# Row sums at the end of a summed-area diagonal kernel: folds on TensorE, weight matmuls on top of an early scan, and fewer load pieces

## The chip, the cores and the metric

One Trainium2 chip; the program runs on one of its cores. The metric is device microseconds of one execution. The timed executions of one kernel agree within about 0.5%; a profiled execution also gives a *span*, the part that the profile covers, about 1.7 to 2 us shorter than the timed value. In the profile PE is TensorE, PEld its weight loads, DVE VectorE, ACT ScalarE, POOL GpSimd and SP SyncE. HBM is the chip's main memory; SBUF and PSUM are memories on the core, and the matmuls of this kernel write to PSUM. Every run told here is of the undisturbed (fast) state.

## The reference

```python
def setup_inputs():
    B, H, W = 4, 4224, 4224
    return {"x": np.random.randn(B, H, W).astype(np.float32)}

def reference(x):
    ps = np.cumsum(np.cumsum(x, axis=1), axis=2)
    diag = np.diagonal(ps, axis1=1, axis2=2)
    return np.cumsum(diag, axis=1).astype(np.float32)
```

The output is tiny (4 x 4224 numbers), but its last value sums over a whole image, so all 285 MB of x must be read once.

## The kernel before

Each of the four images is loaded in strips of 384 rows (3 rows on each of 128 partitions), cast to bf16 by the load. The increment of the diagonal of the summed-area table at index i is a column sum above the diagonal plus a row sum left of it. Column sums come from TensorE (a selector matmul into `d`). Row sums are shared by ScalarE (a copy with an accumulator) and VectorE (a reduce), and are added to `d` through an identity matmul. Two scans of `d` along its 384 columns, a carry between the groups, and y is stored.

The last image is special, because what follows the last load cannot be hidden. Its strips g = 8 and g = 9 arrive in pieces, and the last 384 rows are treated apart: their block near the diagonal is loaded at the very start (`head_a`, `head_b`), the rest (`strip`, 256 rows; `tail`, 128 rows) comes last. Only after the 256 rows' sums are in `d_last` can the two scans over the last 384 rows run.

```python
    DUMP = 2176
    CUTS = {NG - 3: (2176,), NG - 2: (2176, 768)}   # pieces of strips g = 8 and g = 9
# ... cut: constants, scans, between, the loop over the strips
        for q in range(F):
            matmul(d[:ng, q : GW : F], rows[:, :ng, q], ident)
        c12 = smalls.tile([NG, 2, GW], FP32, name="c12")
        scans(d[:ng, :], ng, GW, 0.0, 0.0, c12)
# ... cut: carry matmuls, and lcarry, the carry into the last 384 rows
        cuts = [(1920, T0), (640, 1920), (0, 640)]
        for c0, c1 in cuts:
            nc.gpsimd.dma_start(out=strip[:, :2, c0:c1], in_=src[:, :, c0:c1])
# ... cut: tail pieces
        between(b, ng, c12, carry_ps)                # y of the first ten groups, on VectorE
        lsa = last.tile([P, 3, 2], FP32, name="lsa")
        for i, (c0, c1) in enumerate(cuts):
            act_sum(lsa[:, i, 0:1], strip[:, 0, c0:c1])
            nc.vector.reduce_sum(
                out=lsa[:, i, 1:2], in_=strip[:, 1, c0:c1], axis=AX.X
            )
            for q in range(2):
                matmul(d_last[:, q : 2 * P : 2], lsa[:, i, q : q + 1], ident)

        lc = last.tile([1, 2, GW], FP32, name="lc")
        scans(d_last, 1, GW, lcarry[:, 0:1], lcarry[:, 1:2], lc)
# ... cut: store of 256 values, sums of the tail's pieces into tsum
        nc.vector.reduce_sum(out=ttot, in_=tsum, axis=AX.X)
        matmul(fin, ttot, wtri, start=True)          # the last 128 rows enter by weights
        nc.vector.tensor_add(out=yl, in0=fin, in1=lc[:, 1, 2 * P : GW])
        nc.sync.dma_start(out=out[b, TB:N].unsqueeze(0), in_=yl)
```

Of the kernel before, what the change touches and what calls it, by code (L numbers as in the profile page):

```python
# [17 lines left out]
def kernel(  # L18
# [36 lines left out]

    TB = N - P
    T0 = N - GW
    HB = 2 * P
    head_a = last.tile([P, 2, GW], FP32, name="head_a")
    nc.sync.dma_start(  # L60
        out=head_a, in_=x[LB, T0:TB, T0:N].rearrange("(p f) w -> p f w", f=2)
    )
    head_b = last.tile([P, HB], FP32, name="head_b")
    nc.sync.dma_start(out=head_b, in_=x[LB, TB:N, N - HB : N])

    def load_group(b, g, cuts=()):

        t = strips.tile([P, F, N], BF16, name="strip")
        r0 = g * GW
        src = x[b, r0 : r0 + GW, :].rearrange("(p f) w -> p f w", f=F)  # L70
        hi = N
        for lo in (*cuts, 0):
            if cuts:
                nc.gpsimd.dma_start(out=t[:, :, lo:hi], in_=src[:, :, lo:hi])  # L74
            else:
                nc.gpsimd.dma_start(out=t, in_=src)  # L76
            hi = lo
        return t
# [12 lines left out]
    def upper_masks(f, w):  # L91
# [63 lines left out]
    wtri_i = consts.tile([P, P], I32, name="wtri_i")  # L155
    nc.gpsimd.iota(wtri_i, pattern=[[1, P]], base=1, channel_multiplier=-1)
    wtri = consts.tile([P, P], FP32, name="wtri")
    nc.gpsimd.tensor_copy(out=wtri, in_=wtri_i)
    nc.gpsimd.affine_select(
        out=wtri,  # L160
        in_=wtri,
        compare_op=ALU.is_ge,
        fill=0.0,
        base=0,
        pattern=[[1, P]],
        channel_multiplier=-1,
    )
# [10 lines left out]
    CUTS = {NG - 3: (2176,), NG - 2: (2176, 768)}  # L178
# [12 lines left out]

    hs = last.tile([P, 3], FP32, name="hs")
    hu = last.tile([P, 3], FP32, name="hu")
    hrow = last.tile([P, 3], FP32, name="hrow")
    hmu_a = last.tile([P, 2, GW], BF16, name="hmu_a")
    hmu_b = last.tile([P, P], BF16, name="hmu_b")
    nc.vector.reduce_sum(out=hs[:, 0:2], in_=head_a, axis=AX.X)
    nc.vector.reduce_sum(out=hs[:, 2:3], in_=head_b, axis=AX.X)  # L198
    for k, o, i, m in (
        (0, hmu_a[:, 0, :], head_a[:, 0, :], um2[0]),  # L200
        (1, hmu_a[:, 1, :], head_a[:, 1, :], um2[1]),
        (2, hmu_b, head_b[:, HB - P : HB], um1),
    ):
        nc.vector.scalar_tensor_tensor(
            out=o,
            in0=i,
            scalar=1.0,
            in1=m,
            op0=ALU.mult,
            op1=ALU.mult,  # L210
            accum_out=hu[:, k : k + 1],
        )
    nc.vector.tensor_sub(out=hrow, in0=hs, in1=hu)
# [19 lines left out]
    def between(b, ng, c12, carry_ps):  # L233
        carry = smalls.tile([NG, 2], FP32, name="carry")
        nc.vector.tensor_copy(out=carry[:ng, :], in_=carry_ps[:ng, :])
        y = smalls.tile([NG, GW], FP32, name="y")
        nc.vector.tensor_scalar(
            out=y[:ng, :],
            in0=step[:ng, :],
            scalar1=carry[:ng, 0:1],  # L240
            scalar2=carry[:ng, 1:2],
            op0=ALU.mult,
            op1=ALU.add,
        )
        nc.vector.tensor_add(out=y[:ng, :], in0=y[:ng, :], in1=c12[:ng, 1, :])  # L245
        nc.sync.dma_start(
            out=out[b, : ng * GW].rearrange("(g i) -> g i", i=GW), in_=y[:ng, :]
        )

    for b in range(B):  # L250
# [23 lines left out]
        if not whole:  # L274
            for q in range(2):
                columns(NG - 1, 0, GW, hmu_a[:, q, :])
            columns(NG - 1, GW - P, GW, hmu_b)
            for q in range(2):
                matmul(d_last[:, q : 2 * P : 2], hrow[:, q : q + 1], ident)
# [6 lines left out]
        def sum_pieces(g, parts):  # L286
            nc.vector.reduce_sum(out=rs[:, g, :], in_=parts, axis=AX.X)
            nc.vector.tensor_sub(out=rows[:, g], in0=rs[:, g], in1=ru[:, g])

        for g in range(ng):  # L290
            lo, hi = g * GW, (g + 1) * GW
            cuts = () if whole else CUTS.get(g, ())
            strip = prefetched.pop((b, g), None)
            if strip is None:
                strip = load_group(b, g, cuts)
            if cuts:
                n_parts = 2 * len(cuts) + 2
                parts = last.tile([P, F, n_parts], FP32, name=f"parts{g}")
                c0 = cuts[0]
                ws = c0 + (lo - c0) * 5 // 8 // 32 * 32  # L300
                sa_at = lambda q: parts[:, q, 0:1]
                rs_at = parts[:, :, 1]
            else:
                c0, ws = 0, scalar_cols(g)
                sa_at = lambda q: sa[:, g, q : q + 1]
                rs_at = rs[:, g, :]
            for j in range(g + 1, NG):
                for q in range(F):
                    columns(j, 0, GW, strip[:, q, j * GW : (j + 1) * GW])
            for q in range(F):  # L310
                mu = mup.tile([P, GW], BF16, name="mu")
                nc.vector.scalar_tensor_tensor(  # L312
                    out=mu,
                    in0=strip[:, q, lo:hi],
                    scalar=1.0,
                    in1=um3[q],
                    op0=ALU.mult,
                    op1=ALU.mult,
                    accum_out=ru[:, g, q : q + 1],
                )  # L320
                columns(g, 0, GW, mu)
                if ws > c0:
                    act_sum(sa_at(q), strip[:, q, c0:ws])
            nc.vector.reduce_sum(out=rs_at, in_=strip[:, :, ws:hi], axis=AX.X)  # L324
            if not cuts:
                continue
            k = 2
            for p0, p1 in zip((*cuts[1:], 0), cuts):
                ws = p0 + (p1 - p0) // 2
                for q in range(F):  # L330
                    act_sum(parts[:, q, k : k + 1], strip[:, q, p0:ws])
                nc.vector.reduce_sum(  # L332
                    out=parts[:, :, k + 1], in_=strip[:, :, ws:p1], axis=AX.X
                )
                k += 2
            if g == ng - 2:
                sum_up(0, g)
            sum_pieces(g, parts)

        if whole:  # L340
            sum_up(0, ng)
        for q in range(F):
            matmul(d[:ng, q : GW : F], rows[:, :ng, q], ident)

# [3 lines left out]
        carry_ps = psum_s.tile([NG, 2], FP32, name="carry_ps")  # L348
        matmul(carry_ps[:ng, :], earlier[:ng, :ng], c12[:ng, :, GW - 1], start=True)
        matmul(carry_ps[:ng, 1:2], apart[:ng, :ng], c12[:ng, 0, GW - 1 : GW])  # L350
        if whole:
            between(b, ng, c12, carry_ps)
# [3 lines left out]
        lcarry_ps = psum_s.tile([1, 2], FP32, name="lcarry_ps")  # L356
# [4 lines left out]

        src = x[b, T0:TB, :].rearrange("(p f) w -> p f w", f=2)
        strip = strips.tile([P, F, N], BF16, name="strip")
        cuts = [(1920, T0), (640, 1920), (0, 640)]
        for c0, c1 in cuts:
            nc.gpsimd.dma_start(out=strip[:, :2, c0:c1], in_=src[:, :, c0:c1])  # L366
        tail = strips.tile([P, F, N], BF16, name="strip")
        tcuts = [(2432, N - HB), (1024, 2432), (384, 1024), (0, 384)]
        for c0, c1 in tcuts:
            nc.gpsimd.dma_start(out=tail[:, 0, c0:c1], in_=x[b, TB:N, c0:c1])  # L370

        between(b, ng, c12, carry_ps)

        lsa = last.tile([P, 3, 2], FP32, name="lsa")
        for i, (c0, c1) in enumerate(cuts):
            act_sum(lsa[:, i, 0:1], strip[:, 0, c0:c1])
            nc.vector.reduce_sum(  # L377
                out=lsa[:, i, 1:2], in_=strip[:, 1, c0:c1], axis=AX.X
            )
            for q in range(2):  # L380
                matmul(d_last[:, q : 2 * P : 2], lsa[:, i, q : q + 1], ident)

        lc = last.tile([1, 2, GW], FP32, name="lc")
        scans(d_last, 1, GW, lcarry[:, 0:1], lcarry[:, 1:2], lc)
        nc.sync.dma_start(out=out[b, T0:TB].unsqueeze(0), in_=lc[:, 1, : 2 * P])

        tsum = last.tile([P, 7], FP32, name="tsum")
        nc.vector.tensor_copy(out=tsum[:, 6:7], in_=hrow[:, 2:3])
        fold = psum_s.tile([P, 2 * P], FP32, name="fold")  # L390
        for c0 in range(tcuts[0][0], tcuts[0][1], 2 * P):
            matmul(
                fold,
                ident_h,
                tail[:, 0, c0 : c0 + 2 * P],
                start=c0 == tcuts[0][0],
            )
        nc.vector.reduce_sum(out=tsum[:, 0:1], in_=fold, axis=AX.X)
        k = 1
        for (c0, c1), ws in zip(tcuts[1:], (640, 256, 0)):  # L400
            if ws:
                act_sum(tsum[:, k : k + 1], tail[:, 0, c0 : c0 + ws])
                k += 1
            nc.vector.reduce_sum(  # L404
                out=tsum[:, k : k + 1], in_=tail[:, 0, c0 + ws : c1], axis=AX.X
            )
# [38 lines left out]
```

## Time and profile before

| | before |
|---|---|
| time, median of 3 | 672.1 us (671.86 to 672.22; a fourth run, made later, took 674.20) |
| span of the profiled execution | 670.5 us |
| read from HBM | 285.47 MB, 426 GB/s over the span |
| one strip lands every | 14.95 us, 434 GB/s |
| loads end | 664.25 us (the windows' last quarter with traffic) |
| VectorE / TensorE / ScalarE busy | 39% / 34% / 23% |

The page's line of the HBM traffic (bytes and mean rate):

```profile
HBM read 285.47 MB, written 0.07 MB: 426 GB/s over the span
```

The load stream bounds the kernel for the first 650 us. What a change to the compute can win lies after the last strip. This is the timeline there (start us, duration us, engine, source line, operation, output<-inputs, count, and in brackets the idle time before it and what ended it). L377 are the row sums of the 256 rows, L216 and L224 the two scans over the last 384 rows, L404 the sums of the last 128 rows, L409 their total:

```profile
652.75 1.45 PE L173 MATMUL d<-ident,rows 128*10 128x128 f32 x6 [8.19 <-DVE rows L288]
...
657.90 4.25 DVE L377 TENSOR_REDUCE lsa<-strip 128x1 f32<-128x1920 bf16 x3
...
662.96 1.00 DVE L216 TENSOR_TENSOR_SCAN lc<-ones_row,lcarry,d_last 1x384 f32<-1x384 f32 x1 [0.80 <-PE d_last L173]
...
664.00 1.00 DVE L224 TENSOR_TENSOR_SCAN lc<-ones_row,lcarry,lc 1x384 f32<-1x384 f32 x1
...
665.31 1.85 DVE L404 TENSOR_REDUCE tsum<-strip 128x1 f32<-128x768 bf16 x3
667.26 0.16 DVE L409 TENSOR_REDUCE ttot<-tsum 128x1 f32<-128x7 f32 x1
...
667.57 0.59 PE L173 MATMUL fin<-wtri,ttot 128*1 128x128 f32 x2 [3.38 <-DVE ttot L409]
668.19 0.28 DVE L413 TENSOR_TENSOR yl<-fin,lc 1x128 f32<-1x128 f32 x1 [0.77 <-PE fin L173]
```

VectorE works in one chain from 657.9 to 667.4. Its one wait is the 0.80 us before the first scan, in which TensorE adds VectorE's own last row sums to `d_last`. From the total (667.26) to the end of the span pass 3.2 us.

The windows of the same stretch (start:end, length, busy us and instructions of each engine, granted TensorE clock as a share of full speed, DMA share, GB/s):

```profile
core 0: us, PE busy (x) PEld busy (x) DVE busy (x) ACT busy (x) POOL busy (x), PEclk, DMA share, GB/s
...
658.50:661.90 3.40, 1.43 (x7) 0.58 (x8) 3.40 (x3) 1.76 (x4) 0.00 (x0) 0.50 1.09 208
661.90:665.30 3.40, 2.29 (x11) 1.03 (x9) 2.56 (x5) 1.34 (x4) 0.00 (x0) 0.70 0.34 56
665.30:668.70 3.40, 0.59 (x2) 0.11 (x2) 2.30 (x6) 0.00 (x0) 0.00 (x0) 0.80 0.00 0
```

The clock is at half in the first of these windows, released in the course of the second and back at half near the end of the third.

### The profile page before, as it was taken

The page shows a single profiled execution, that of the slowest core. Times are in us where ns is not written, and L with a number is a line of the kernel's source. Part 1 is how long each engine was busy: PE and PEld are TensorE (multiplying, and loading weights), DVE is VectorE, ACT ScalarE, POOL GpSimd, SP SyncE. Part 2 cuts the span into 40 slices and gives each one's busy share as a digit, 9 for nine tenths or more (in the row PEclk, how much of TensorE's full clock was granted, in tenths as well). Part 3 has the DMA queues.
Part 4 walks back from the last instruction along what each step waited for, and adds up shares of the span by engine and source line. Part 5 has one row for each costly group of instructions (what it writes and reads, how often), then busy time and mean ns, then how long its engine had stood idle before and what let it go on. Part 6 is the DMA issues. An engine that isn't in the chain of part 4 may idle for free.

```text
span 670.5 us, 2653 instructions
## 1 busy us (share of the span) xinstructions
PE 226.3 (34%) x860; PEld 96.0 (14%) x860; DVE 261.3 (39%) x374; ACT 155.7 (23%) x263; POOL 35.4 (5%) x73
## 2 busy tenths in 40 slices
PE   0444443211145543221125543222214533332313
PEld 0211211000022211100012221110002211111101
DVE  2223334344613333334472222333456222233767
ACT  0001222233301112223330111222342011122553
POOL 5000000000000000000000000000000010000100
PEclk9977766555577766566557766766655776766656
DMA  9999999999999999999999999999999999999996
GB/s 199 220 218 217 218 218 218 216 218 218 215 218 218 218 217 216 215 216 216 215 216 217 216 218 218 216 216 218 217 216 219 216 218 217 218 216 206 215 212 114
DMA packets 9814, 143.22 MB, mean 214 GB/s; under 512 B 925, under 2 KB 2250, under 8 KB 4554
## 3 DMA queue, kind: packets, MB, share of 16 engines
q0 software_dynamic: 9296, 142.48, 99.6%
q1 hardware_dynamic: 506, 0.59, 0.3%
q8 instruction: 6, 0.10, 0.1%
q14 instruction: 6, 0.05, 0.0%
HBM read 285.47 MB, written 0.07 MB: 426 GB/s over the span
## 4 chain that ended last, share of the span: by engine, by line
another core or an unknown queue 67%; ACT 22%; DMA 7%; DVE 2%; issue 1%; PE 1%; POOL 0%; ACTq 0%; DVEq 0%; POOLq 0%
ACT dump L183 22%; DMA strip<-in_x_dram 7%; DVE lsa L377 1%; DVE tsum L404 0%; PE d L173 0%; PE d_last L173 0%; POOL strip L76 0%; DVE lc L216 0%; DVE lc L224 0%; DVE c L224 0%; DVE c L216 0%; ACTq L183 0%; PE fin L173 0%; DVE y L245 0%
## 5 line engine op out<-in xcount | busy, mean ns | idle before, releaser
L173 PE MATMUL d<-strip,sel 128*11 128x384 bf16 x630 | 174.7, 457 | 346.0 <-DMA strip<-in_x_dram 346.0
L183 ACT ACTIVATE dump<-strip 128x640 bf16<-128x640 bf16 (+14 forms) x131 | 142.3, 1086 | 508.1 <-DMA strip<-in_x_dram 505.3
L312 DVE SCALAR_TENSOR_TENSOR mu<-strip,um 128x384 bf16<-128x384 bf16 x129 | 65.2, 555 | 374.1 <-DMA strip<-in_x_dram 374.1
L173 PEld LDWEIGHTS <-sel 128*11 128x11 bf16 (+1 forms) x792 | 90.2, 114 | 519.1 <-issue 497.1
L324 DVE TENSOR_REDUCE rs<-strip 128x3 f32<-128x1152 bf16 (+10 forms) x41 | 158.2, 3858 | 0.0
L173 PE MATMUL d<-mu,sel 128*11 128x384 bf16 x129 | 38.1, 404 | 40.6 <-DVE mu L312 40.6
L76 POOL DMA_DIRECT2D strip<-in_x_dram x41 | 22.0, 539 | 509.8 <-PE d L173 240.8
L183 ACT ACTIVATION_READ_ACCUMULATOR dump<-strip 128x1 f32 x131 | 24.4, 186 | 0.0
L173 PE MATMUL d<-ident,rows 128*11 128x128 f32 (+1 forms) x24 | 5.8, 414 | 28.1 <-DVE rows L284 19.9
L173 PE MATMUL d_last<-strip,sel 128*1 128x384 bf16 x30 | 9.0, 425 | 12.1 <-DMA strip<-in_x_dram 12.1
L312 DVE DVE_READ_ACCUMULATOR mu<-strip,um 128x1 f32 x129 | 10.6, 82 | 0.0
L332 DVE TENSOR_REDUCE parts<-strip 128x3 f32<-128x3264 bf16 (+2 forms) x3 | 7.3, 2421 | 5.0 <-DMA strip<-in_x_dram 5.0
L173 PEld LDWEIGHTS d<-ident,rows 128*11 128x11 f32 (+1 forms) x24 | 2.7, 127 | 32.6 <-DVE rows L284 15.0
L216 DVE TENSOR_TENSOR_SCAN c<-ones_row,d 11x384 f32<-11x384 f32 (+1 forms) x4 | 3.8, 942 | 6.3 <-PE d L173 6.3
L74 POOL DMA_DIRECT2D strip<-in_x_dram x5 | 3.8, 762 | 34.5 <-PE d L173 27.3
L198 DVE TENSOR_REDUCE hs<-head_b 128x1 f32<-128x256 f32 x1 | 0.4, 419 | 13.0 <-DMA head_b<-in_x_dram 13.0
L324 DVE TENSOR_REDUCE parts<-strip 128x3 f32<-128x2208 bf16 (+1 forms) x2 | 5.3, 2650 | 0.0
L366 POOL DMA_DIRECT2D strip<-in_x_dram x3 | 2.1, 713 | 42.7 <-DMA strip<-in_x_dram 42.7
L377 DVE TENSOR_REDUCE lsa<-strip 128x1 f32<-128x1920 bf16 (+2 forms) x3 | 4.3, 1465 | 0.0
L173 PE MATMUL d_last<-ident,lsa 128*1 128x128 f32 x12 | 3.0, 406 | 3.3 <-DVE lsa L377 3.0
L224 DVE TENSOR_TENSOR_SCAN c<-ones_row,c 11x384 f32<-11x384 f32 (+1 forms) x4 | 3.8, 946 | 0.1
L173 PE MATMUL carry_ps<-c,earlier 11*11 11x2 f32 (+1 forms) x8 | 0.7, 159 | 8.4 <-DVE c L224 8.4
(62 smaller groups left out, 35.8 us busy)
## 6 DMA issues: line engine op xcount, KB each, us to landing
strip<-in_x_dram POOLq DMA_DIRECT2D x41, 3168.0 KB, 82.7
strip<-in_x_dram POOLq DMA_DIRECT2D x2, 1536.0 KB, 76.0
strip<-in_x_dram POOLq DMA_DIRECT2D x1, 1632.0 KB, 83.2
strip<-in_x_dram POOLq DMA_DIRECT2D x1, 1056.0 KB, 80.1
strip<-in_x_dram POOLq DMA_DIRECT2D x1, 960.0 KB, 64.3
strip<-in_x_dram POOLq DMA_DIRECT2D x1, 640.0 KB, 52.7
strip<-in_x_dram POOLq DMA_DIRECT2D x1, 576.0 KB, 74.9
head_a<-in_x_dram SPq DMA_DIRECT2D x1, 384.0 KB, 3.7
```

The costliest lines, as they stand in the source:

```text
L74: nc.gpsimd.dma_start(out=t[:, :, lo:hi], in_=src[:, :, lo:hi])
L76: nc.gpsimd.dma_start(out=t, in_=src)
L173: nc.tensor.matmul(o, lhsT=lhsT, rhs=rhs, start=start, stop=False, skip_group_check=True)
L183: nc.scalar.activation(out=dump[:, :w], in_=src, func=ACT.Copy, accum_out=acc)
L198: nc.vector.reduce_sum(out=hs[:, 2:3], in_=head_b, axis=AX.X)
L216: nc.vector.tensor_tensor_scan(out=c12[:rows, 0, :width], data0=ones_row[:rows, :width], data1=d, initial=init1, op0=ALU.mult, op1=ALU.add,)
L224: nc.vector.tensor_tensor_scan(out=c12[:rows, 1, :width], data0=ones_row[:rows, :width], data1=c12[:rows, 0, :width], initial=init2, op0=A ...
L312: nc.vector.scalar_tensor_tensor(out=mu, in0=strip[:, q, lo:hi], scalar=1.0, in1=um3[q], op0=ALU.mult, op1=ALU.mult, accum_out=ru[:, g, q ...
L324: nc.vector.reduce_sum(out=rs_at, in_=strip[:, :, ws:hi], axis=AX.X)
L332: nc.vector.reduce_sum(out=parts[:, :, k + 1], in_=strip[:, :, ws:p1], axis=AX.X)
L366: nc.gpsimd.dma_start(out=strip[:, :2, c0:c1], in_=src[:, :, c0:c1])
L377: nc.vector.reduce_sum(out=lsa[:, i, 1:2], in_=strip[:, 1, c0:c1], axis=AX.X)
```

## The change

The intent: get the last rows' scans off the end. They now run early, on what is known without the late row sums; those enter afterwards through matmuls with fixed weights (`w2`, `w1`), because the double cumulative sum is linear and a row sum at row r adds (i + 1 - r) times itself to index i. The row sums themselves are shared by three engines: TensorE folds wide blocks into 160 or 256 columns by identity matmuls, ScalarE and VectorE take the rest. Strips g = 8 and g = 9 arrive whole, the end in 5 pieces instead of 7; the 256 rows' near-diagonal block (`diag_a`) comes in after strip g = 0 of the last image; y of the first ten groups moves to GpSimd.

The core of the diff, cut (the load helper, the constants and the bookkeeping are left out):

```diff
     DUMP = 2176
-    CUTS = {NG - 3: (2176,), NG - 2: (2176, 768)}
# ... cut
+            if not whole and g == ng - 1:
+
+                wp, ws = 1280, 1280 + 1536
+                fold9 = psum_s.tile([P, F, 160], FP32, name="fold")
+                fold_in(fold9, strip, 0, wp, 160)
# ... cut: diag_a and its sums at g == 0 and g == 1
+            fold_a = psum_s.tile([P, 2, 256], FP32, name="fold_a")
+            A_SHARES = [(768, 1152), (768, 640)]
+            (c0, c1), (wp, wa) = acuts[0], A_SHARES[0]
+            fold_in(fold_a, strip[:, :2], c0, c0 + wp, 256)
# ... cut: ScalarE's and VectorE's shares of the first piece
-        between(b, ng, c12, carry_ps)
-
-        lsa = last.tile([P, 3, 2], FP32, name="lsa")
-        for i, (c0, c1) in enumerate(cuts):
-            act_sum(lsa[:, i, 0:1], strip[:, 0, c0:c1])
-            nc.vector.reduce_sum(
-                out=lsa[:, i, 1:2], in_=strip[:, 1, c0:c1], axis=AX.X
-            )
-            for q in range(2):
-                matmul(d_last[:, q : 2 * P : 2], lsa[:, i, q : q + 1], ident)
-
+        between(b, ng, c12, carry_ps, nc.gpsimd)
         lc = last.tile([1, 2, GW], FP32, name="lc")
         scans(d_last, 1, GW, lcarry[:, 0:1], lcarry[:, 1:2], lc)
# ... cut: second piece of the 256 rows
+        nc.vector.reduce_sum(out=asum[:, :, 5], in_=fold_a, axis=AX.X)
+        arows = last.tile([P, 2], FP32, name="arows")
+        nc.vector.reduce_sum(out=arows, in_=asum, axis=AX.X)
# ... cut
+        for q in range(2):
+            ar = arows[:, q : q + 1]
+            matmul(fin_b, ar, w2[q][:, 2 * P : GW], start=q == 0)
+            matmul(fin_a, ar, w2[q][:, 0 : 2 * P], start=q == 0)
# ... cut: sums of the tail into tsum
         nc.vector.reduce_sum(out=ttot, in_=tsum, axis=AX.X)
-        matmul(fin, ttot, wtri, start=True)
-        yl = last.tile([1, P], FP32, name="yl")
-        nc.vector.tensor_add(out=yl, in0=fin, in1=lc[:, 1, 2 * P : GW])
-        nc.sync.dma_start(out=out[b, TB:N].unsqueeze(0), in_=yl)
+        matmul(fin_b, ttot, w1)
+        yl = last.tile([1, GW], FP32, name="yl")
+        for fin, c0, c1 in ((fin_a, 0, 2 * P), (fin_b, 2 * P, GW)):
+            nc.vector.tensor_add(out=yl[:, c0:c1], in0=fin, in1=lc[:, 1, c0:c1])
+            nc.sync.dma_start(
+                out=out[b, T0 + c0 : T0 + c1].unsqueeze(0), in_=yl[:, c0:c1]
+            )
```

## The prediction

> **What bounds it now.** The load stream. The page's HBM line: 285.47 MB read, 426 GB/s over the span. The timeline shows one full strip (384 rows, 6.49 MB of fp32) landing every 14.95 us (590.1, 605.04, 620.0), so 434 GB/s while it runs. The Trainium skill ("DMA: Bandwidth & Descriptors", Specifications) gives a fabric ceiling of 435 GB/s; this trace agrees. VectorE is 39% busy (section 1). At 434 GB/s everything takes an estimated 658 of the 670.5 us.  The rest is the start (first strip at 20.3 us) and the end: the windows show the load rate falling after 662.0 and ending at 664.25; the span ends 6.2 us later.
>
> **The end now** (timeline). VectorE hardly rests from 656.7: three row reduces (4.25 us, at one column per ns), scans over the last 384 rows (662.96 to 665.0), then the tail's reduces (665.31 to 667.16) with data there by about 664.6. Then the total (667.26), weight matmul (to 668.16), add (0.28), store (issued 668.50, span end 670.5): 3.2 us after the total starts.
>
> **What changes.**
> 1. Same bytes. Two strips arrive whole; after them 5 pieces instead of 7; packets are larger. The windows show 217 GB/s for whole strips but 215 (620 to 640 us) and 212 (640 to 660) for pieces: estimated 0.3 to 0.4 us earlier end of loads.
> 2. The last whole strip (g=9) is ready only near 651.0 (now its last piece at 650.32), because 0.2 MB moved ahead of it. Its sums are then one block: masks 1.44, reduce of 3,072 columns 3.35 (2,592 took 2.85), small sums and the fold's reduce 1.5, 768 columns 0.93, wait for the row matmuls 0.65.
> 3. The last rows' scan leaves the end: its inputs need only the early data, so it runs at about 661.7 to 663.75. VectorE's row reduces shrink from 3,840 columns to 768+256 plus one 512-column fold reduce.
> 4. New on TensorE: folds (8 of 480, 6 of 512, 5 of 256 columns) and four fp32 weight matmuls (2 of 128, 2 of 256 columns). From the d_last matmuls (0.24 us per pass of 128 columns at half clock) those four cost an estimated 2.6 us at half clock, 1.3 us at full, and stand ahead of the final one.
> 5. y of the first groups goes to GpSimd, off the path.
>
> Adding VectorE's work from 651.0 (15.1 us) puts the total at about 666.1, 1.1 to 1.2 us earlier than now. VectorE remains the last chain; data would allow about 664.8. The end after the total stays about 3.2 us if TensorE has full clock at 665 to 667 us. The Trainium skill ("TensorE: Matmul & The Clock Gate", Part 1) says the default is throttled and activity releases it. Before's windows agree (89% busy at 660.5 to 663.9, then clock 1.0). The folds should keep it released; if not, the weight matmuls end near 667.7 and the gain vanishes.
>
> **Prediction:** 671.0 us (range 670.0 to 672.1); faster by over 2%: 0.5%, same 99%, slower 0.5%.
>
> **Right if:** strip landings still 14.95 us apart; loads end at 663.7 to 664.2; the last-row scans end before 664.3; the total starts at 665.7 to 666.6; the final stretch from total to end 3.1 to 3.4 us.
>
> **Wrong if:** TensorE runs at half clock at 665 us and the weight matmuls, not VectorE, end last (about 672); the folds of g=9 delay the first scan; GpSimd's y delays the store queue; fewer pieces help the load rate more than estimated, or the first loads change the start.

## The result and the profile after

| | before | after |
|---|---|---|
| median of 4 timed runs | 672.16 us (671.86 to 674.20) | 671.78 us (671.36 to 673.04) |
| ratio after / before | | 0.9991, 95% interval 0.9967 to 1.0015 |
| span of the profiled execution | 670.5 us | 670.4 us |
| loads end | 664.25 us | about 663.7 us |
| grand total starts | 667.26 us | 665.91 us |
| last add starts | 668.19 us | 668.09 us |

A ratio here and below is the mean time of one kernel's fast runs over that of the other's of the same rounds, so it is not quite the ratio of the medians.

The grand total is 1.35 us earlier, as was hoped, and the last add is only 0.1 us earlier. The bytes are the same; the page's line for after:

```profile
HBM read 285.47 MB, written 0.07 MB: 426 GB/s over the span
```

The timeline of the end (L187 at 651.04 is the first instruction on the landed strip g = 9; L207 and L215 are the scans; L383 forms the 256 rows' sums, L405 the total; `fin_a` and `fin_b` are the weight matmuls, two passes each, as for every fp32 matmul in these traces, where the bf16 folds have one; L409 are the last adds):

```profile
651.04 0.56 DVE L187 SCALAR_TENSOR_TENSOR mu<-strip,um 128x384 bf16<-128x384 bf16 x1 [7.96 <-DMA strip<-in_x_dram]
...
657.43 0.83 PE L169 MATMUL d<-ident,rows 128*10 128x128 f32 x6 [1.55 <-DVE rows L269]
...
660.91 1.00 DVE L207 TENSOR_TENSOR_SCAN lc<-ones_row,lcarry,d_last 1x384 f32<-1x384 f32 x1
...
661.78 0.98 POOL L236 TENSOR_TENSOR y<-y,c 10x384 f32<-10x384 f32 x1
661.95 1.63 DVE L215 TENSOR_TENSOR_SCAN lc<-ones_row,lcarry,lc 1x384 f32<-1x384 f32 x1
...
664.59 0.17 DVE L383 TENSOR_REDUCE arows<-asum 128x2 f32<-128x12 f32 x1
...
664.90 0.59 PE L169 MATMUL fin_b<-w,arows 128*1 128x128 f32 x2 [0.78 <-DVE arows L383]
...
665.29 1.06 PE L169 MATMUL fin_a<-w,arows 128*1 128x256 f32 x2
...
665.91 0.16 DVE L405 TENSOR_REDUCE ttot<-tsum 128x1 f32<-128x6 f32 x1
666.14 0.63 PE L169 MATMUL fin_b<-w,arows 128*1 128x128 f32 x2
...
666.57 1.06 PE L169 MATMUL fin_a<-w,arows 128*1 128x256 f32 x2
...
667.42 0.63 PE L169 MATMUL fin_b<-w,ttot 128*1 128x128 f32 x2
...
667.66 0.41 DVE L409 TENSOR_TENSOR yl<-fin_a,lc 1x256 f32<-1x256 f32 x1 [1.59 <-PE fin_a L169]
668.09 0.28 DVE L409 TENSOR_TENSOR yl<-fin_b,lc 1x128 f32<-1x128 f32 x1
```

The total is ready at 666.07. But TensorE is still on the four weight matmuls of the 256 rows, which began at 664.90, and only at 667.42 does the first pass of the total's own matmul start. In the trace they run one after the other, in the order of the program. The waits of 664 to 673 us (who waited for whom: us in total, times, longest) name it:

```profile
DVE yl L409 <- PE fin_a L169: 1.6, 1, 1.6
```

The windows say why those matmuls are slow:

```profile
655.00:658.50 3.50, 1.95 (x13) 0.86 (x12) 3.24 (x9) 2.76 (x5) 0.00 (x0) 1.00 1.09 217
658.50:661.90 3.40, 1.59 (x14) 0.58 (x13) 2.85 (x5) 2.22 (x6) 0.77 (x2) 0.99 1.01 193
661.90:665.30 3.40, 1.62 (x8) 0.80 (x8) 3.26 (x7) 1.69 (x5) 0.87 (x1) 0.50 0.18 29
665.30:668.70 3.40, 2.75 (x9) 0.87 (x7) 1.36 (x5) 0.00 (x0) 0.00 (x0) 0.50 0.02 5
```

The clock was granted in full from 655.0 to 661.9 and is half from there. From start to start `fin_a` of 256 columns takes 0.85 us and `fin_b` of 128 columns about 0.4; from the first start to the end that the profile gives for the last (667.63) the four take 2.7 us. A second new thing stands in the timeline: L215, the second last-row scan, takes 1.63 us, although the same scan took 1.00 in before. GpSimd's add of y (L236, 661.78 to 662.76) lies beside it.

### The profile page after: what moved, and what is told of

Read it like the earlier page. It is cut to its first block, busy times and chain, and to the rows that moved or that the text cites. A ratio compares the mean times of both kernels' runs of the same rounds, so it can differ in the third digit from the quotient of the medians.

```text
span 670.4 us, 2644 instructions
## 1 busy us (share of the span) xinstructions
PE 227.5 (34%) x865; PEld 96.3 (14%) x865; DVE 256.0 (38%) x370; ACT 152.9 (23%) x247; POOL 36.5 (5%) x77
## 3 DMA queue, kind: packets, MB, share of 16 engines
HBM read 285.47 MB, written 0.07 MB: 426 GB/s over the span
## 4 chain that ended last, share of the span: by engine, by line
another core or an unknown queue 53%; DVE 35%; DMA 7%; PE 3%; issue 1%; POOL 0%; DVEq 0%; POOLq 0%
DVE rs L297 23%; DVE mu L187 9%; DMA strip<-in_x_dram 7%; PE d L169 3%; DVE c L215 1%; DVE c L207 1%; PE fin_a L169 0%; DVE lc L215 0%; POOL strip L64 0%; DVE y L236 0%; PE carry_ps L169 0%; PE fin_b L169 0%; DVE lc L207 0%; DVE rows L269 0%
## 5 line engine op out<-in xcount | busy, mean ns | idle before, releaser
L178 ACT ACTIVATE dump<-strip 128x640 bf16<-128x640 bf16 (+12 forms) x123 | 140.2, 1140 | 511.0 <-DMA strip<-in_x_dram 508.4
L187 DVE SCALAR_TENSOR_TENSOR mu<-strip,um 128x384 bf16<-128x384 bf16 x129 | 65.2, 555 | 395.6 <-DMA strip<-in_x_dram 395.6
L297 DVE TENSOR_REDUCE rs<-strip 128x3 f32<-128x1152 bf16 (+11 forms) x43 | 167.1, 3886 | 0.0
L64 POOL DMA_DIRECT2D strip<-in_x_dram x43 | 23.0, 537 | 535.5 <-PE d L169 268.2
L178 ACT ACTIVATION_READ_ACCUMULATOR dump<-strip 128x1 f32 x123 | 22.9, 186 | 0.0
L187 DVE DVE_READ_ACCUMULATOR mu<-strip,um 128x1 f32 x129 | 10.7, 83 | 0.0
L207 DVE TENSOR_TENSOR_SCAN c<-ones_row,d 11x384 f32<-11x384 f32 (+1 forms) x4 | 3.8, 942 | 4.8 <-PE d L169 4.7
L169 PE MATMUL fold<-strip,ident_h 128*128 128x480 bf16 (+1 forms) x13 | 4.5, 518 | 1.5 <-DMA strip<-in_x_dram 1.5
L215 DVE TENSOR_TENSOR_SCAN c<-ones_row,c 11x384 f32<-11x384 f32 (+1 forms) x4 | 3.8, 946 | 0.1
L330 POOL DMA_DIRECT2D strip<-in_x_dram x3 | 1.6, 538 | 22.1 <-PE d L169 14.2
L169 PEld LDWEIGHTS <-ident_h 128*128 128x128 bf16 x19 | 2.1, 124 | 4.7 <-issue 4.1
L85 POOL TENSOR_SCALAR_AFFINE_SELECT um<-um 128x384 bf16<-128x384 bf16 (+1 forms) x6 | 2.6, 477 | 0.1
L326 POOL DMA_DIRECT2D strip<-in_x_dram x2 | 1.4, 709 | 13.5 <-PE d L169 13.5
L169 PE MATMUL fin_a<-w,arows 128*1 128x256 f32 x4 | 2.1, 631 | 0.0
```

Source lines behind the costliest of these rows:

```text
L64: nc.gpsimd.dma_start(out=t, in_=x[b, r0 : r0 + GW, :].rearrange("(p f) w -> p f w", f=F))
L85: nc.gpsimd.affine_select(out=um, in_=um, compare_op=ALU.is_gt, fill=0.0, base=-q, pattern=[[1, w]], channel_multiplier=-f,)
L169: nc.tensor.matmul(o, lhsT=lhsT, rhs=rhs, start=start, stop=False, skip_group_check=True)
L178: nc.scalar.activation(out=dump[:, :w], in_=src, func=ACT.Copy, accum_out=acc)
L187: nc.vector.scalar_tensor_tensor(out=o, in0=i, scalar=1.0, in1=m, op0=ALU.mult, op1=ALU.mult, accum_out=acc,)
L207: nc.vector.tensor_tensor_scan(out=c12[:rows, 0, :width], data0=ones_row[:rows, :width], data1=d, initial=init1, op0=ALU.mult, op1=ALU.add,)
```

## The experiments

Because the landing of the last strip moved by up to 1.6 us from one profile to the next (650.08 to 651.68 over all variants of the changed kernel), I compare two stretches that don't contain it: the *chain*, from the first instruction on the landed strip g = 9 to the start of the last add, and the *close*, from there to the end of the span. For the changed kernel, the chain is 668.09 - 651.04 = 17.05 us and the close 670.4 - 668.1 = 2.3 us.

The runs were made on three chips, four runs and before on each: after_again to noweights, warm_yafter to before_warm, and warm_again to drain.

Theory A: the four weight matmuls at half clock are the last chain. Theory B, the rival: GpSimd's y stretches VectorE's scan, and VectorE is what ends late.

| run | ratio to before (95%) | median us | landing | chain | close |
|---|---|---|---|---|---|
| after_again | 0.9996 (0.9984 to 1.0009) | 671.52 | 650.51 | 17.06 | 2.3 |
| warm | 0.9976 (0.9964 to 0.9989) | 670.18 | 650.08 | 15.72 | 2.4 |
| ylate | 0.9989 (0.9975 to 1.0003) | 671.47 | 651.23 | 16.80 | 2.3 |
| noweights (wrong) | 0.9973 (0.9961 to 0.9986) | 670.33 | 650.32 | 16.43 | 2.3 |
| warm_yafter | 1.0003 (0.9990 to 1.0017) | 672.52 | 651.68 | 15.14 | 3.5 |
| yafter | 0.9991 (0.9979 to 1.0004) | 671.51 | 650.21 | 15.97 | 2.7 |
| pieces (on before) | 1.0078 (1.0065 to 1.0092) | 677.32 | | | |
| before_warm (on before) | 1.0022 (1.0009 to 1.0034) | 673.64 | | | |
| warm_again | 0.9978 (0.9965 to 0.9992) | 670.12 | 650.10 | 15.72 | 2.4 |
| rows_first | 0.9972 (0.9959 to 0.9984) | 670.26 | 650.15 | 15.92 | 2.4 |
| warm_yact | 0.9975 (0.9963 to 0.9988) | 670.28 | 650.37 | 16.78 | 2.4 |
| drain | 1.0008 (0.9996 to 1.0021) | 672.54 | 650.20 | 17.05 | 3.1 |

Every run has five rounds. Every ratio is within 2% of before; what separates the theories is the chain in the profiles, with the ratios beside it. All results passed the comparison with the reference; that of noweights did too, though its last values are wrong by construction, so the comparison is too coarse to catch it.

### after_again: the changed kernel unaltered

> The changed kernel unaltered, as the common measure for the others on this chip. Both theories: ratio to before 0.998 to 1.000, span about 670.0 to 670.5. It also shows whether the half clock in the last 7 us repeats. Theory A (TensorE at half clock makes the four weight matmuls, 2.7 us, the last chain) expects that a profile with the half clock at 665 us again ends near 670.4, and one with full clock near 669.0. Theory B (GpSimd working on y stretches the last scan from 1.00 to 1.63 us, and VectorE is what ends late) expects the second last-row scan at 1.6 us again and the same end whatever the clock.

Measured: 671.52 us, ratio 0.9996. The half clock repeated (0.50 from 661.9 to 668.7), the scan took 1.64 us, and the chain was 17.06 us against 17.05: what follows the landing is the same to 0.01 us. The span is 0.6 us shorter than in the first profile because the strip landed 0.5 us earlier.

### warm and warm_again: full clock at the end

Idle matmuls into an unused PSUM tile fill TensorE's gaps. They add work and change no result.

```diff
+            spare = psum_d.tile([NG, GW], FP32, name="d")
+
+            def keep_busy(n):
+                for _ in range(n):
+                    matmul(spare, selector(0), um3[0], start=True)
+
# ... keep_busy(5) after the first fold_a, keep_busy(6) after the second, keep_busy(3) after fold_b
```

> Idle matmuls of 384 columns into an unused PSUM tile fill TensorE's gaps (5, 6 and 3 of them) so that the clock stays released. Theory A: clock 1.0 from 658 to 667 us, the four weight matmuls take about 1.3 us instead of 2.7, the last add starts 1.2 to 1.4 us earlier after the loads' end, span about 669.0, ratio to the unaltered changed kernel 0.998. Theory B alone: no change, or up to 0.5 us longer, because the matmuls only stand in the way.

The windows of warm, then its timeline, to be read against those of after:

```profile
658.50:661.90 3.40, 2.62 (x20) 1.08 (x19) 2.85 (x5) 1.66 (x4) 1.63 (x2) 1.00 0.98 187
661.90:665.30 3.40, 2.63 (x17) 1.24 (x17) 3.02 (x8) 1.68 (x4) 0.00 (x0) 1.00 0.15 22
665.30:668.70 3.40, 0.35 (x3) 0.05 (x2) 0.61 (x2) 0.00 (x0) 0.00 (x0) 1.00 0.02 5
```

```profile
663.65 0.17 DVE L390 TENSOR_REDUCE arows<-asum 128x2 f32<-128x12 f32 x1
...
663.96 0.38 PE L169 MATMUL fin_b<-w,arows 128*1 128x128 f32 x2 [0.72 <-DVE arows L390]
...
664.82 0.59 PE L169 MATMUL fin_a<-w,arows 128*1 128x256 f32 x2
664.96 0.16 DVE L413 TENSOR_REDUCE ttot<-tsum 128x1 f32<-128x6 f32 x1
...
665.27 0.38 PE L169 MATMUL fin_b<-w,ttot 128*1 128x128 f32 x2
...
665.80 0.27 DVE L417 TENSOR_TENSOR yl<-fin_b,lc 1x128 f32<-1x128 f32 x1
```

Measured: full clock in all three windows; the four weight matmuls take 665.41 - 663.96 = 1.5 us instead of 2.7; the total's matmul starts 0.15 us after the total instead of 1.35; the chain is 15.72 us, 1.33 shorter. VectorE's part did not change: the total starts 14.88 us after the landing, against 14.87 in after. All of the gain lies behind the total (0.84 us from there to the last add instead of 2.18). The scan is stretched as before (1.64 us at 661.00), so theory B alone cannot account for the end.

> The clock test once more, on whatever chip comes, with the changed kernel's other variants beside it. Theory A: full clock from before 660 us to the end, 15.7 us from the landing of the last strip (first mask of g=9) to the last add, as in the first run and against 17.05 in both profiles of the unaltered changed kernel; ratio to before 0.997 to 0.999, spread by when the last strip lands. If the first run was luck of the landing: 0.9995.

Measured on another occasion: the same chain to 0.01 us, ratio 0.9978. Theory A stands: the same instructions in the same order, with extra work added, end 1.3 us earlier at full clock. The timed gain over the unaltered kernel on the same chip (671.52 - 670.18 = 1.34 us) agrees with the chain, though some of it may be the landing, which was 0.4 us earlier in the profile of warm, and the intervals of the two ratios just overlap.

### noweights: the four matmuls left out

```diff
-        for q in range(2):
-            ar = arows[:, q : q + 1]
-            matmul(fin_b, ar, w2[q][:, 2 * P : GW], start=q == 0)
-            matmul(fin_a, ar, w2[q][:, 0 : 2 * P], start=q == 0)
# ... the first last add takes lc twice instead of fin_a; the total's matmul has start=True
```

> Wrong result on purpose: the four weight matmuls of the 256 rows are left out, the final one of the last 128 rows stays. Theory A: the final matmul starts right after the grand total (about 666.2 instead of 667.4) even at half clock, the last add starts near 666.9 instead of 668.1, span 1.2 us shorter, about 669.2. Theory B alone: the grand total is what ends late, so at most 0.3 us.

```profile
665.82 0.16 DVE L400 TENSOR_REDUCE ttot<-tsum 128x1 f32<-128x6 f32 x1
...
666.13 0.58 PE L169 MATMUL fin_b<-w,ttot 128*1 128x128 f32 x2 [3.22 <-DVE ttot L400]
...
666.75 0.28 DVE L404 TENSOR_TENSOR yl<-fin_b,lc 1x128 f32<-1x128 f32 x1 [0.45 <-PE fin_b L169]
```

Measured: ratio 0.9973. The total's matmul starts at 666.13, 0.15 us after the total is ready, at half clock (0.50 in the last window); from the start of the total to the last add 0.93 us pass instead of 2.18. The chain is 16.43, only 0.6 us shorter; the rest of the expected 1.2 went earlier, where this profile's clock was at half from 656.7 and the row matmuls of `d` took 1.45 us instead of 0.83. So the matmuls are on the path, and the clock acts at more than one place.

### ylate and yafter: GpSimd away from the scan

ylate computes y on VectorE after the total; yafter leaves it on GpSimd but after the two scans.

```diff
# ylate
-        between(b, ng, c12, carry_ps, nc.gpsimd)
+        # (after matmul(fin_b, ttot, w1))
+        between(b, ng, c12, carry_ps, nc.vector)
# yafter
-        between(b, ng, c12, carry_ps, nc.gpsimd)
         lc = last.tile([1, 2, GW], FP32, name="lc")
         scans(d_last, 1, GW, lcarry[:, 0:1], lcarry[:, 1:2], lc)
+        between(b, ng, c12, carry_ps, nc.gpsimd)
```

> y of the first ten groups goes back to VectorE, but after the grand total, where VectorE waits for TensorE; GpSimd computes nothing beside the scans. Theory B: the second last-row scan is 1.00 us again instead of 1.63, the row sums and with them the weight matmuls start 0.6 us earlier, span about 669.8. If GpSimd does not stretch the scan: it stays 1.6 us and nothing moves.

> GpSimd's y held back until after the scans, nothing else. The second scan takes 1.00 us instead of 1.63, so the weight matmuls start 0.6 us earlier after the last early sum. If the clock is half again they still end last and the end comes 0.6 us earlier: ratio to before about 0.9985. If the stretched scan costs nothing at the end: same as the unaltered changed kernel, 0.9996.

The scan in each of the two, by its timeline line:

```profile
662.52 1.00 DVE L215 TENSOR_TENSOR_SCAN lc<-ones_row,lcarry,lc 1x384 f32<-1x384 f32 x1
```

```profile
661.11 1.00 DVE L215 TENSOR_TENSOR_SCAN lc<-ones_row,lcarry,lc 1x384 f32<-1x384 f32 x1
```

Measured: 1.00 us in both, against 1.63, 1.64 and 1.64 in after, after_again and warm. GpSimd's add stretches the scan; that half of theory B is shown. Its worth at the end is less clear. In ylate the chain is 0.25 us shorter, not 0.6, because in this profile the clock was at half from 657.9 already and TensorE's early work was slower. In yafter it is 1.08 us shorter, more than the scan's 0.63, because this profile's clock came back at about 665.2, in the middle of the weight matmuls. Neither ratio is clear of the unaltered kernel's.

### warm_yafter: both cures, and what came instead

The edits of warm and of yafter together.

> The idle matmuls of the clock test, and GpSimd's y held back until after the two last-row scans. If GpSimd stretches only the scan, the scan is 1.00 us, the VectorE reduces after it keep their 0.38, 0.67, 0.17, 0.41, 0.48 and 0.41 us, and from the last early sum to the last add 8.9 us pass instead of 9.5 (clock test) and 10.9 (unaltered): ratio to before about 0.9967. If GpSimd stretches any VectorE work beside it, the reduces get longer instead and nothing is gained over the clock test (0.9976).

Measured: the chain is 15.14 us, the shortest of all, 0.58 below warm, as expected; the reduces that now lie beside GpSimd's work took 0.40, 0.67, 0.17, 0.41 and 0.48 us, so they are not stretched; and the time is 672.52 us, worse than the unaltered kernel. Part of that is the landing (651.68 us in the profile, the latest of all). The other part is the close, 3.5 us instead of 2.4. The closing instructions show where it comes from. These are the lines of the drains at the end of the program (engine, count, shortest/median/longest in ns, first and last start) in after, then in warm_yafter:

```profile
L438 POOLq DRAIN  x3: 40/108/5119, 661.7 to 670.1; - x3
L438 SPq DRAIN  x3: 7/7/7, 669.5 to 669.8; - x3
```

```profile
L446 POOLq DRAIN  x3: 40/99/5119, 664.5 to 670.1; - x3
L446 SPq DRAIN  x3: 7/7/7, 668.4 to 669.8; - x3
```

GpSimd's first drain takes 5,119 ns in both. It starts with GpSimd's last computing instruction: at 661.7 in after, so it is over at 666.8, long before SyncE's first drain at 669.5. In warm_yafter y is late, the drain runs from 664.5 to 669.6, and SyncE, ready at 668.4, goes on only at 669.8. So a late instruction on GpSimd holds the end of the program, although y's store, the only user of its result, was issued at 665.5 already. The same shows in yafter, where SyncE went on 0.4 us later than it would have, which explains its close of 2.7 us.

### drain: that cost by itself

```diff
         matmul(fin_b, ttot, w1)
+        junk = last.tile([P, 1], FP32, name="junk")
+        nc.gpsimd.tensor_copy(out=junk, in_=ttot)
```

> The changed kernel with one added GpSimd copy of 128 numbers after the grand total, which nothing waits for. If GpSimd's closing drain of 5.12 us after its last computing instruction lies on the end of the program, the copy near 666.2 us keeps the end until about 671.3 plus 0.7: span about 672, 1.6 us longer, ratio about 1.002. If the drain costs nothing at the end: 0.9995, as the changed kernel.

```profile
L440 POOLq DRAIN  x3: 40/99/4307, 665.3 to 670.1; - x3
```

Measured: the chain is 17.05, exactly the unaltered kernel's, and the close 3.1 us instead of 2.3. The drain was 4.31 us here, from 665.3 to 669.6, so less than the expected 5.12; SyncE was ready at 668.7. The difference is the instruction itself: the add takes 0.98 us and the copy 0.19, and from the end of either to the end of the drain some 4.1 us pass. The ratio, 1.0008, is 0.12 to 0.17% above the unaltered kernel's 0.9991 and 0.9996; the intervals overlap. The direction is as expected, the size (0.8 us in the profile) half of the 1.6 expected.

### rows_first: the matmuls earlier instead of faster

```diff
-        lc = last.tile([1, 2, GW], FP32, name="lc")
-        scans(d_last, 1, GW, lcarry[:, 0:1], lcarry[:, 1:2], lc)
# ... reduces of the 256 rows' second piece and of fold_a, as before
         nc.vector.reduce_sum(out=arows, in_=asum, axis=AX.X)
+        lc = last.tile([1, 2, GW], FP32, name="lc")
+        scans(d_last, 1, GW, lcarry[:, 0:1], lcarry[:, 1:2], lc)
```

> No idle matmuls; VectorE forms the 256 rows' sums before the two last-row scans instead of after them, so the weight matmuls start earlier. Theory A: they start as soon as the tail's fold is done (about 12.9 us after the last strip lands instead of 13.9) and are out of the way about 0.8 us earlier even at half clock: 16.2 to 16.4 us from landing to last add instead of 17.05, ratio about 0.9987. If VectorE were the last chain, the order of its own work would change nothing: 17.0.

```profile
660.90 0.98 POOL L236 TENSOR_TENSOR y<-y,c 10x384 f32<-10x384 f32 x1
...
661.47 0.99 DVE L207 TENSOR_TENSOR_SCAN lc<-ones_row,lcarry,d_last 1x384 f32<-1x384 f32 x1
...
662.50 1.01 DVE L215 TENSOR_TENSOR_SCAN lc<-ones_row,lcarry,lc 1x384 f32<-1x384 f32 x1
...
663.17 0.58 PE L169 MATMUL fin_b<-w,arows 128*1 128x128 f32 x2
...
666.07 0.27 DVE L409 TENSOR_TENSOR yl<-fin_b,lc 1x128 f32<-1x128 f32 x1
```

Measured: the row sums are ready at 661.6, the weight matmuls start 13.0 us after the landing instead of 13.9 and the chain is 15.92 us, shorter than the expected 16.2 to 16.4. VectorE does the same work in another order, which would change nothing if VectorE ended last. Two other things helped and are not separated by this run. The second scan now starts after GpSimd's add is over and takes 1.01 us; the first scan, which lies beside the add, takes 0.99 and is not stretched. And the clock returned to full near 665.3, for the last of the matmuls. The ratio is 0.9972, the lowest of the correct kernels here, with no added work.

### pieces: one part of the change alone, on the kernel before

```diff
-    CUTS = {NG - 3: (2176,), NG - 2: (2176, 768)}
+    CUTS = {}
# ... and sum_up(0, ng) for every image
```

> One part of the change alone, on the kernel before: the strips g=8 and g=9 arrive whole. Loads should end 0.1 to 0.3 us earlier; but the last strip's row sums, 3,840 columns a row, then start only when all of it is there: VectorE's reduce is 5,760 columns (about 6.2 us) after 650.3, so the rows are summed near 658.3 instead of 652.7 and the end comes 4 to 6 us later, ratio about 1.007. If the pieces only cost transfer time: 0.9995.

```profile
651.08 6.15 DVE L324 TENSOR_REDUCE rs<-strip 128x3 f32<-128x5760 bf16 x1
...
657.80 1.45 PE L173 MATMUL d<-ident,rows 128*10 128x128 f32 x6 [6.11 <-DVE rows L284]
```

Measured: 5 us slower, as expected. The whole strip's reduce of 5,760 columns takes 6.15 us, the row matmuls start at 657.80 instead of 652.75, and everything behind shifts by as much. The strip g = 9 was complete 0.7 us earlier (649.63 against 650.32) and the last load packet 0.8 us (663.36 against 664.20), more than the expected 0.1 to 0.3, which doesn't help where VectorE ends last. The folds and ScalarE's larger share win part of this back in the changed kernel: its row matmuls start 6.4 us after the landing (657.43 against 651.04), here 8.2.

### before_warm: idle matmuls in the kernel before

Eight after the row matmuls, two after the carries, four after each of the first two row-sum updates, eight after the fold.

> The same idle matmuls in the kernel before. Theory A says the clock matters only where TensorE ends last, and before VectorE does: TensorE's part after the grand total is one matmul, 0.2 us shorter at full clock, and the row matmuls of the last rows another 0.2 to 0.3; ratio 0.9992 to 0.9998. If a released clock helps any end of this kind: 0.998, as much as in the changed kernel.

Measured: 1.5 us slower; the expectation missed. The clock did not stay up: 0.96 in the window from 655 to 658.5, then 0.53 and 0.50. At half clock the groups of four stood for 1.3 us each in front of the matmuls that feed `d_last`, and the first last-row scan began at 664.78 instead of 662.96. The run shows what idle matmuls cost in the wrong place; it doesn't show what full clock would do for before, and that stays open.

### warm_yact: half of y on ScalarE

```diff
# shortened; for the last image alone
-        eng.tensor_scalar(out=y[:ng, :], in0=step[:ng, :], scalar1=carry[:ng, 0:1], scalar2=carry[:ng, 1:2], ...)
+        nc.scalar.activation(out=y[:ng, :], in_=step[:ng, :], func=ACT.Identity, scale=carry[:ng, 0:1], bias=carry[:ng, 1:2])
```

> The clock test, with the first half of y on ScalarE, so that GpSimd's add starts 0.4 us earlier and lies beside the first last-row scan more than the second. If the add is what stretches a scan that reads SBUF, the second scan takes 1.2 to 1.4 us instead of 1.63 and the last add comes 0.2 to 0.4 us earlier after the landing (15.3 to 15.5 us instead of 15.7). If GpSimd's add stretches any scan, the first one grows instead and the sum stays.

Measured: inconclusive. The add still lay beside the second scan (662.19 to 663.18 beside a scan of 1.67 us), so the test of the scan didn't come about. The clock in this profile fell back to half from 656.7 to 660.1 (mean 0.75 and 0.76 in the windows from 655 and from 658.5), the five idle matmuls then stood in front of the carry matmuls, and the chain was 16.78 us. The ratio, 0.9975, is that of warm; the other four runs, with spans of 668.2 to 669.3 us against 669.5, were perhaps not caught so, which isn't shown.

## Why the prediction was right, and which term of it was off

**The time.** Predicted 671.0 us, range 670.0 to 672.1, same; measured 671.78, and 671.52 on another chip, same. The range held, but by luck as far as the mechanism goes: it also covered the prediction's own way to be wrong (about 672), and that is what came. Of the five conditions under "right if" one failed: the final stretch was 4.5 us instead of 3.1 to 3.4. The point was 0.5 to 0.8 us too low, which is half or more of the 1.1 us of gain that it forecast, and the gain itself isn't clear of the noise.

**The loads.** Same bytes (285.47 MB in both pages), strips 14.95 us apart (606.17, 621.13, 636.09, 651.04). The loads ended 0.5 us earlier (the last packet of the load queue at 663.69, in before at 664.20); 0.3 to 0.4 was predicted. Traffic after that is y's store. It didn't matter, since the loads didn't end last. One estimated size is off without a consequence.

**VectorE's chain to the total.** Predicted to start at 666.1 from a landing at 651.0, 15.1 us; measured 665.91 from 651.04, 14.87 us. Two errors cancelled. The wait for the row matmuls was put at 0.65 us and was 0.05, because the clock was at full there; the second scan took 0.63 us more than the 1.00 that I had carried over from before, because GpSimd's add ran beside it. I had called y on GpSimd "off the path"; its result is, its effect on VectorE isn't.

**The step that failed: from the total to the end.** The prediction put this at 3.2 us "if TensorE has full clock at 665 to 667 us" and held that the folds should keep the clock released. Measured: 670.4 - 665.9 = 4.5 us at half clock. The folds did release the clock, from 655.0 to 661.9, but did not keep it: it fell 3 us before it was needed. The mis-sized term is the four weight matmuls: 1.3 us assumed, 2.7 us measured (the prediction's own figure for half clock was 2.6). They started at 664.90, when `arows` was ready, and so the total's matmul came at 667.42 instead of 666.2. That is where 1.2 us of the total's lead of 1.35 went; not VectorE but TensorE ended last. The mechanism stood in the prediction as its first way to be wrong, with about 672 us; the experiments warm, warm_again and noweights show it.

**How the Trainium skill was used.** "TensorE: Matmul & The Clock Gate", Part 1, says that the default is throttled and activity releases it, and before's trace agreed: TensorE 89% busy from 660.5 to 663.9, then clock 1.0. The same section's table lets the clock fall after an idle window of about 3.4 us. I took from it that folds and carries a microsecond or two apart would hold it. The trace after disagrees: in the window from 658.5 to 661.9 TensorE was busy for 1.59 us and no gap was over 1.5 us, and the clock fell at 661.9. In rows_first it fell at 662.0 after 1.09 us of work from 658.5, in after_again at 661.5 after 1.53 us of work from 658.0. The measurement decides: the absence of long gaps isn't enough.

The traces say more than I took from them. In all fourteen, every stretch of one clock inside the span is a multiple of 3.41 us long; in after the steps begin at 655.03, 658.44, 661.85 and 665.27, in warm at 655.40, so they aren't tied to the program. Counted over all these steps, some 2,600, full clock was never kept after one with less than 1.42 us of TensorE work and never lost after one with more than 1.79, and half clock never ended after less than 2.61 us nor went on after more than 2.70 (after: 1.86 us from 655.03, kept; 1.65 from 658.44, lost; noweights: 1.79 from 660.01, lost). Where the steps lie against the landing differs from profile to profile (one begins 2.9 us after it in noweights, 4.0 in after, 5.3 in warm), which may be why the early clock of noweights, ylate and warm_yact was another; no run here tests it.

**The stretched scan.** "SBUF — State Buffer", Who interferes with whom, says that a DVE instruction with two SBUF inputs contends with a GpSimd instruction that reads SBUF, and one with at most one SBUF input outside the two-port modes doesn't. The second scan, which reads both its inputs from SBUF, took 1.63 us beside GpSimd's add and 1.00 without; the first, which has one input in PSUM, took 0.99 to 1.00 us either way.

**What stays open.** The landing of the last strip varied between 650.08 and 651.68 us over eleven profiles of the changed kernel and its variants, and that of the first strip between 19.5 and 21.8; late first strips went with late last ones (21.78 with 651.68, 19.49 with 650.20). In three profiles of before and its variants the first strip came between 20.0 and 20.3. Before's runs were tighter in the same session (671.72 to 672.39 in nine, against 671.27 to 673.45 in five of the changed kernel), though one of its first four took 674.20. No experiment tells whether the new shape of the first load does this. Nor was the half clock observed in unprofiled runs, where only the span's mean is known.

## What to carry to other kernels

When serial work moves from one engine to another near the end of a program, cost it at the slow state of the receiving engine, and ask what that engine did in the few microseconds before; here the same four matmuls were 1.5 or 2.7 us. Moving their start (sums first, scans second) gave as much as keeping the clock up with idle matmuls (ratios 0.9972 and 0.9976 to 0.9978) and adds no work, though in that run the unstretched scan and the clock's return helped too. Work sent to GpSimd "off the path" can still come back twice, through a VectorE instruction that runs beside it and through the end of the program.

## What the Trainium skill lacked or had wrong

- "TensorE: Matmul & The Clock Gate", Part 1 and HAM oscillation: the clock is said to fall after an idle window of about 3.4 us, and the rule given is no idle gaps over about 3.4 us. That is incomplete: here it fell after 3.41 us with 1.65 us of work (after), 1.53 (after_again) or 1.09 us (rows_first), with no gap over 1.5 us; with 2.59 us of work from 658.81 (warm) it stayed. The page's next section does tell of short, frequent idles that make the clock swing, but the page gives no busy share for either change; over the fourteen traces the limit lay between 1.42 and 1.79 us for losing full clock and between 2.61 and 2.70 us for gaining it.
- No page gives the cost of GpSimd's drain at the end of a program. It took 5.12 us from the start of GpSimd's last computing instruction (4.31 us after a small copy) and held the end in three runs: by about 1.1 us in warm_yafter, 0.8 in drain and 0.4 in yafter. "VectorE: DVE Perf Modes", The DRAIN you can't avoid, speaks of about 12 ns on all engines, but for the drains of the runtime's own start and end; the one here stands at a line of the kernel's file (L438 in after). What it waits for stays open: where GpSimd computes nothing late it also ran until 666.2 (ylate, from 606.5) and 666.7 (before, from 647.7).
- "SBUF — State Buffer", Who interferes with whom, was right about the contended scan; it calls the shared ports an exclusive lock and gives no time for such a case. Here it cost 0.63 us on a scan of 1.00 us beside an add of 0.98 us, of which 0.81 us were left when the scan started.
